# Swapping products between the two rounds of a seven-product down projection

## The chip, the cores and the metric

The kernel runs on one core of a Trainium2 chip: TensorE (PE) for matmuls and transposes, VectorE (DVE), ScalarE (ACT), GpSimd (POOL), and SyncE (SP), whose queue issues most DMAs. The metric is the device time of one execution in microseconds. A profiled execution also has a span, from its first to its last instruction.

## The reference

A decoder block on 512 tokens of width 1024: an RMS norm, one wide input projection, sliding-window attention and a gated linear recurrence side by side, their merge, an output projection with residual, and then the part at issue, a SwiGLU network of hidden width 2816 followed by a last norm:

```python
u = rmsnorm(h, norm_ffn_g[layer])
z = (jax.nn.silu(jnp.einsum('bsd,df->bsf', u, w_ffn_gate[layer]))
     * jnp.einsum('bsd,df->bsf', u, w_ffn_up[layer]))
h = h + jnp.einsum('bsf,fd->bsd', z, w_ffn_down[layer])
return rmsnorm(h, norm_final_g)
```

Everything is float32.

## The kernel before, in words

Every float32 operand is split into a high part in a rounded format (a ScalarE copy, line 109 for weights) and a low part, the rest (a VectorE subtraction, line 113). A product is then three matmuls: high by high, high by low, low by high.

Weights come through the class `Weights`. Its units of 1 MB are loaded into two buffers `raw` (lines 56 to 74), in one fixed list; each unit is two grains, and `get` splits grains two ahead of use into three buffers `wh`/`wl`.

The down projection z (512 x 2816) by w_d (2816 x 1024) is done as a fast 2 x 2 block product: the blocks are the two token halves, two neighbouring blocks of 128 hidden rows (a pair, p = 0 to 10), and the two output halves. Seven products per pair stand in place of eight. Each takes a form of z (a11, a12, a22, and sums s2, s3, n1, n4) and a form of the weights (b11, b12, b21, b22, and sums y1 to y4), and accumulates over the pairs in PSUM. With two token tiles of 128 and three matmuls of 512 columns a product is six matmuls per pair.

Seven products need fourteen PSUM banks and there are eight, so there are two rounds. Round 1, n1y1, a12b21 and n4b22, lies inside the gate/up stream: for each p the list `ffn` (lines 189 to 192) puts two gate projections, the round-1 products of p-1, then two up projections; the products of the last two pairs stand at the end. `up_` (lines 906 to 922) multiplies gate and up, forms the sums of z in `z8` and splits them: three forms (h1, l1) for round 1 at once, four (zh, zl) kept for round 2. Round 2, lines 964 to 983, reads w_d again for a11b11, s3y3, s2y2 and a22y4. `sums` (lines 117 to 128) forms the weight sums in place on VectorE: one per pair in round 1 (y1), three in round 2 (y3, y2, y4).

Between the rounds, lines 950 to 957, ScalarE copies the six banks of round 1 to SBUF and GpSimd adds them onto hn, the residual, in eight additions. Then the pool is released and round 2 takes all eight banks. The last TAIL_P = 2 pairs have their four grains split into buffers of their own (lines 970 and 971) and their matmuls traced product by product (`tail`). Lines 1021 to 1041 add the four results onto hn, take the squares of each row block for the last norm, scale and store.

The order of instructions on each engine is made when the program is built: a scheduler lists them by a simulated timeline, keeping dependences; `tc.issue_after(x)` makes an instruction follow x on its engine. On the chip each engine keeps that order. So matmuls of several products of the tail are mixed in the trace.

Of the kernel before, what the change touches and what calls it, by code (L numbers as in the profile page):

```python
# [22 lines left out]
P = 128  # L23
# [8 lines left out]
C_K, C_V, C_HQ, C_HF, C_HI, C_HG, C_GA, C_GB = (  # L32
    1024, 1152, 1280, 2304, 3328, 4352, 5376, 6400)
NP = NF // 2
TAIL_P = 2
WARM = 28
AHEAD = 2

# [3 lines left out]
class Weights:  # L42
# [13 lines left out]
    def load(self, u):  # L56
        if u >= len(self.units) or u in self.raw:
            return
        kind, w, c0 = self.units[u]
        t = self.pool.tile([P, 2048], F32, tag="raw", bufs=2, name=f"raw{u}")  # L60
        if kind in ("r1", "r2"):
            self.nc.sync.dma_start(
                t.rearrange("p (f n) -> p f n", f=2),
                w[c0 * P:(c0 + 2) * P, :].rearrange("(f p) n -> p f n", p=P))
        elif kind == "n":
            k0, n0 = c0
            self.nc.sync.dma_start(
                t.rearrange("p (k n) -> p k n", k=4),
                w[k0 * P:(k0 + 4) * P, n0:n0 + 512].rearrange("(k p) n -> p k n", p=P))
        else:  # L70
            self.nc.sync.dma_start(
                t.rearrange("p (k n) -> p k n", k=KD),
                w[:, c0:c0 + 256].rearrange("(k p) n -> p k n", p=P))
        self.raw[u] = t
# [10 lines left out]
    def split(self, i, pool=None, bufs=3, high=None, low=None, low_after=None):  # L85
        u, kind, half = self.grans[i]
        self.load(u)
        if u:
            self.load(u + 1)
        nc, raw = self.nc, self.raw[u]  # L90
        if kind == "c":
            src = raw.rearrange("p (k n) -> p k n", k=KD)[:, :, half * P:(half + 1) * P]
            shape = dict(k=KD)
        else:
            n = 256 if kind == "k" else 512
            src = raw[:, half * 1024:(half + 1) * 1024].rearrange("p (k n) -> p k n", n=n)
            shape = dict(n=n)
        size = 1024
        if kind in ("r1", "r2"):
            self.sums(kind, half, raw)  # L100
            if kind == "r1" and not half:
                src, size = src[:, 0:1, :], 512
# [12 lines left out]
        self.done = i + 1  # L115

    def sums(self, kind, half, raw):

        b11, b12, b21, b22 = (raw[:, 512 * i:512 * i + 512] for i in range(4))
        add = lambda o, i0, i1: self.nc.vector.tensor_tensor(o, i0, i1, ALU.add)  # L120
        if kind == "r1":
            if not half:
                add(b11, b11, b12)
        elif not half:
            add(b12, b12, b22)
        else:
            add(b22, b11, b12)
            add(b21, b21, b22)

    def get(self, limit=None):  # L130
        i = self.pos
# [8 lines left out]
def block_kernel(ctx: ExitStack, tc: tile.TileContext, x, norm_mix_g, w_in, b_in,  # L140
# [722 lines left out]
    def psg(name):  # L863
        return psum.tile([P, S], F32, tag="g", bufs=2, name=name)
# [38 lines left out]
    def halves(v):  # L903
        return v.rearrange("p (a c) -> p a c", a=2)

    def up_(p):
        z8 = fp.tile([P, 8, 256], F32, tag="z8", bufs=1, name="z8")
        n1, n4, a12, a11, s2, s3, a22, a21 = (z8[:, i, :] for i in range(8))
        for a in range(2):
            dst = z8.rearrange("p (a b) c -> p a b c", a=2)[:, :, 3 - a, :]  # L910
            tt(dst, halves(fproject()), halves(gates_of[p][a]), ALU.mult)  # L911
            if not a:
                tt(s3, a21, a11, ALU.subtract)
        tt(n1, a21, a22, ALU.subtract)
        tt(s2, a11, n1, ALU.subtract)
        tt(n4, a12, s2, ALU.subtract)
        h1 = fp.tile([P, 3, 256], F32R, tag="h1", bufs=2, name="f1h")
        l1 = fp.tile([P, 3, 256], F32R, tag="l1", bufs=2, name="f1l")
        for h, l, src in ((h1, l1, z8[:, 0:3, :]), (zh[:, p], zl[:, p], z8[:, 3:7, :])):
            act(h, src, AF.Copy)  # L920
            tt(l, src, h.bitcast(F32), ALU.subtract)
        forms1[p] = h1, l1

    def product(ps, ah, al, wh, wl, first, last):
        for i in range(2):
# [3 lines left out]

    def round1(p):  # L930
        h, l = forms1.pop(p)
        for names in (("n1y1",), ("a12b21", "n4b22")):
            wh, wl = W.get(limit=stream_end)
            for b, n in enumerate(names):
                f = dict(n1y1=0, n4b22=1, a12b21=2)[n]
# [23 lines left out]
    psum = newpool("psd", "left", bass.MemoryType.PSUM)  # L959
    acc = {n: [psum.tile([P, S], F32, name=f"{n}_{i}") for i in range(2)]  # L960
           for n in ("a11b11", "s3y3", "s2y2", "a22y4")}
    form = dict(a11b11=0, s2y2=1, s3y3=2, a22y4=3)

    for p in range(NP - TAIL_P):
        for names in (("a11b11", "s3y3"), ("a22y4", "s2y2")):
            wh, wl = W.get(limit=stream_end)
            for b, n in sorted(enumerate(names), key=lambda v: v[1] == "a22y4"):
                product(acc[n], zh[:, p, form[n]], zl[:, p, form[n]], wh[:, b], wl[:, b],
                        p == 0, False)
    for g in range(2 * TAIL_P):  # L970
        W.split(stream_end + 1 + g, wd, 2 * TAIL_P)

    def tail(n, i):

        for p in range(NP - TAIL_P, NP):
            g = stream_end + 1 + 2 * (p - NP + TAIL_P) + (n in ("s2y2", "a22y4"))
            wh, wl = W.ready[g]
            b = int(n in ("s3y3", "s2y2"))
            ts = slice(i * P, (i + 1) * P)
            ah, al = zh[:, p, form[n], ts], zl[:, p, form[n], ts]  # L980
            for m, (x, w) in enumerate(((ah, wh), (ah, wl), (al, wh))):
                pe.matmul(acc[n][i], x, w[:, b], start=False, stop=p == NP - 1 and m == 2)
        return acc[n][i]

    jks = {}
# [1 line left out]
    def start_row(t):  # L987
        s2 = dp.tile([P, 5], F32, tag="s2", bufs=4, name="s2d")
        dve.memset(s2[:, 4:5], EPS)
        jks[t] = s2  # L990
# [30 lines left out]
    vs = []  # L1021
    for i in range(2):
        p1 = tail("a11b11", i)
        start_row(i)
        v = dp.tile([P, S], F32, tag="v", bufs=2, name="v")
        act(v, p1, AF.Copy)
        add_side(i, 0, p1)
        vs.append(v)
    for i in range(2):
        tt(vs[i], tail("s2y2", i), vs[i], ALU.subtract)  # L1030
        add_side(i, 1, vs[i])
        finish_row(i, 1)
    for i in range(2):
        t = 2 + i
        tt(vs[i], tail("s3y3", i), vs[i], ALU.add)
        start_row(t)
        add_side(t, 1, vs[i])
        tt(hn[:, t, 0:S], hn[:, t, 0:S], vs[i], ALU.subtract)
    for i in range(2):
        add_side(2 + i, 0, tail("a22y4", i))  # L1040
        finish_row(2 + i, 0)
    for pl in (dp, zpool, top):
        pl.release()
    for pl in (wd, hpool, wpool, cst):
# [32 lines left out]
```

## Time and profile before

| | us |
|---|---|
| runs | 918.30 median, 917.96 to 920.95 (3 runs) |
| profiled execution, its own time | 919.07 |
| its span | 917.2 |
| PE busy | 885.4 (97%) |
| DVE busy | 554.4 (60%) |
| ACT busy | 398.3 (43%) |
| POOL busy | 163.1 (18%) |
| mean granted TensorE clock | 0.988 of full speed |

Busy is the time in which an engine had an instruction in work; matmuls are pipelined, so a busy PE says that matmuls followed each other, not how fast. The gate/up stream runs from about 541 to 823, round 2 from about 829 to 899, and what follows to 917.2 is the closing of the rows.

### The profile page before, as it was taken

What the parts mean: (1) busy time and instruction counts of PE and PEld (TensorE: products, weight loads), DVE (VectorE), ACT (ScalarE), POOL (GpSimd) and SP (SyncE); (2) the same over time, 40 slices, a digit from 0 to 9 for tenths busy, and PEclk for the clock granted to TensorE, in tenths of its full rate; (3) what the DMA queues carried; (4) which work ended last, traced back from release to release, by engine and by line L of the source; (5) the groups of instructions that cost most, each with busy time, mean ns of one, the idle gap of its engine ahead of it and who ended that gap; (6) DMA issues with size and microseconds to landing.
All of it is one profiled execution on the core that took longest, in us unless ns stands there. A gap on an engine that the chain in (4) does not pass through costs nothing.

```text
span 917.2 us, 11242 instructions
## 1 busy us (share of the span) xinstructions
PE 885.4 (97%) x4410; PEld 747.8 (82%) x4410; DVE 554.4 (60%) x833; ACT 398.3 (43%) x648; POOL 163.1 (18%) x156
## 2 busy tenths in 40 slices
PE   8999999999999999999999999999999999997992
PEld 7888889898888988888888878888888888875881
DVE  5677877556484846545434454555656556467777
ACT  6566766654452726125222343333333323243334
POOL 3013533300000000000000002233333122225004
PEclk9999999999999999999999999999999999999996
DMA  7221211323222131312252222443343333434542
GB/s 255 93 93 47 92 51 43 110 74 113 71 92 85 33 114 60 125 46 93 93 194 94 85 86 92 138 137 102 128 138 95 135 117 113 138 94 138 204 139 91
DMA packets 74465, 97.26 MB, mean 106 GB/s; under 512 B 1866, under 2 KB 64428, under 8 KB 74412
## 3 DMA queue, kind: packets, MB, share of 16 engines
q1 hardware_dynamic: 73820, 95.48, 31.9%
q10 hardware_dynamic: 592, 1.05, 0.3%
q8 instruction: 35, 0.57, 0.3%
q14 instruction: 18, 0.15, 0.0%
HBM read 94.43 MB, written 2.10 MB: 105 GB/s over the span
## 4 chain that ended last, share of the span: by engine, by line
PE 89%; DVE 4%; DMA 3%; SPq 1%; issue 1%; ACT 0%; POOL 0%; POOLq 0%; DVEq 0%; ACTq 0%
PE ps_big L385 13%; PE ps_big L386 13%; PE ps_big L387 13%; PE ps_f L385 8%; PE ps_f L387 8%; PE ps_f L386 8%; DMA raw<-in_w_ffn_down_dram 3%; PE ps_v L396 2%; PE ps_v L397 2%; PE ps_v L395 2%; PE ps_o L396 2%; PE ps_o L397 2%; PE ps_o L395 2%; PE pv L521 1%; PE n4b L928 1%; PE a12b L928 1%
## 5 line engine op out<-in xcount | busy, mean ns | idle before, releaser
L109 ACT ACTIVATE wh<-raw 128x1024 fp32r<-128x1024 f32 (+1 forms) x169 | 174.0, 1032 | 372.8 <-PE ps_f L386 145.9
L113 DVE TENSOR_TENSOR wl<-raw,wh 128x1024 fp32r<-128x1024 f32 (+1 forms) x169 | 211.6, 1253 | 112.0 <-ACT wh L109 111.7
L385 PE MATMUL ps_big<-uh,wh 128*128 128x512 f32 x376 | 148.8, 396 | 0.0
L386 PE MATMUL ps_big<-ul,wh 128*128 128x512 f32 x376 | 147.8, 393 | 0.0
L387 PE MATMUL ps_big<-uh,wl 128*128 128x512 f32 x376 | 147.7, 393 | 0.0
L385 PE MATMUL ps_f<-u2h,wh 128*128 128x512 f32 x352 | 137.1, 390 | 0.8 <-DVE R L880 0.8
L387 PE MATMUL ps_f<-u2h,wl 128*128 128x512 f32 x352 | 137.0, 389 | 0.0
L386 PE MATMUL ps_f<-u2l,wh 128*128 128x512 f32 x352 | 136.9, 389 | 0.0
L387 PEld LDWEIGHTS ps_big<-uh,wl 128*128 128x128 f32 x376 | 70.7, 188 | 14.2
L386 PEld LDWEIGHTS ps_big<-ul,wh 128*128 128x128 f32 x376 | 70.8, 188 | 13.6
L385 PEld LDWEIGHTS ps_big<-uh,wh 128*128 128x128 f32 x376 | 70.7, 188 | 13.5
L385 PEld LDWEIGHTS ps_f<-u2h,wh 128*128 128x128 f32 x352 | 66.1, 188 | 15.1 <-DVE R L880 1.6
L386 PEld LDWEIGHTS ps_f<-u2l,wh 128*128 128x128 f32 x352 | 66.1, 188 | 13.8
L387 PEld LDWEIGHTS ps_f<-u2h,wl 128*128 128x128 f32 x352 | 66.1, 188 | 13.8
L899 POOL TENSOR_TENSOR zg<-zg,sgf 128x512 f32<-128x512 f32 x22 | 37.9, 1723 | 194.2 <-ACT sgf L158 194.2
L120 DVE TENSOR_TENSOR raw<-raw 128x512 f32<-128x512 f32 x44 | 33.7, 765 | 38.8 <-DMA raw<-in_w_ffn_down_dram 38.1
L279 POOL TENSOR_TENSOR r<-ss,neghalf 128x4 f32<-128x4 f32 x8 | 10.1, 1260 | 232.8 <-DVE ss L278 232.8
L911 DVE TENSOR_TENSOR z<-ps_f,zg 128x512 f32<-128x512 f32 x22 | 15.1, 688 | 37.9 <-PE ps_f L387 37.9
L900 POOL TENSOR_TENSOR zg<-zg,R 128x512 f32<-128x512 f32 x22 | 36.7, 1669 | 1.7
L395 PE MATMUL ps_v<-wh,uh 128*128 128x256 f32 x128 | 36.5, 285 | 0.0
L396 PE MATMUL ps_v<-wl,uh 128*128 128x256 f32 x128 | 36.3, 284 | 0.0
L397 PE MATMUL ps_v<-wh,ul 128*128 128x256 f32 x128 | 36.2, 284 | 0.0
(299 smaller groups left out, 1615.8 us busy)
## 6 DMA issues: line engine op xcount, KB each, us to landing
raw<-in_w_in_dram SPq DMA_DIRECT2D x27, 1024.0 KB, 5.2
raw<-in_w_ffn_down_dram SPq DMA_DIRECT2D x22, 1024.0 KB, 4.9
raw<-in_w_ffn_gate_dram SPq DMA_DIRECT2D x11, 1024.0 KB, 5.1
raw<-in_w_ffn_up_dram SPq DMA_DIRECT2D x11, 1024.0 KB, 5.2
raw<-in_w_branch_attn_dram SPq DMA_DIRECT2D x4, 1024.0 KB, 5.3
raw<-in_w_branch_hgrn_dram SPq DMA_DIRECT2D x4, 1024.0 KB, 4.8
raw<-in_w_out_dram SPq DMA_DIRECT2D x4, 1024.0 KB, 4.8
xt<-in_x_dram SPq DMA_DIRECT2D x4, 512.0 KB, 6.5
```

The costliest lines, as they stand in the source:

```text
L109: nc.scalar.activation(hv, src, AF.Copy)
L113: (low or nc.vector).tensor_tensor(lv, src, hv.bitcast(F32), ALU.subtract)
L120: add = lambda o, i0, i1: self.nc.vector.tensor_tensor(o, i0, i1, ALU.add)
L385: pe.matmul(ps, wh[:, k, :], ah[:, k, :], start=k == 0, stop=False)
L386: pe.matmul(ps, wh[:, k, :], al[:, k, :], start=False, stop=False)
L387: pe.matmul(ps, wl[:, k, :], ah[:, k, :], start=False, stop=k == KD - 1)
L395: pe.matmul(ps, ah[:, k0 + k, ts], wh[:, k, :], start=first and k == 0, stop=False)
L396: pe.matmul(ps, ah[:, k0 + k, ts], wl[:, k, :], start=False, stop=False)
L397: pe.matmul(ps, al[:, k0 + k, ts], wh[:, k, :], start=False, stop=last and k == nk - 1)
L899: pool_e.tensor_tensor(zg, zg, sg, ALU.mult)
L900: pool_e.tensor_tensor(zg, zg, R, ALU.mult)
L928: pe.matmul(ps[i], x[:, ts], w, start=first and n == 0, stop=last and n == 2)
```

## The change

Round 1 now computes s3y3, a22y4 and s2y2, whose weights need three sums per pair; round 2 computes a11b11, n1y1, a12b21 and n4b22, which need one. The weight rows of round 2 are loaded as single blocks of 128 rows, two DMAs of 512 KB per unit, so that for the last three pairs (TAIL_P = 3) the three even blocks come first, then the odd ones. The round-1 products of pair 9 move between the gate and up projections of pair 10; those of pair 10 follow the last up projection directly, and for that pair the forms of z are split one by one. Between the rounds eight GpSimd additions become ten on VectorE. bc, the broadcast of the row scale, uses a bank of s2y2. The products of the tail are tied to the order in which they are traced, accumulator by accumulator, and the closing of the rows follows that order.

```diff
-TAIL_P = 2
+TAIL_P = 3
...
+        elif kind == "r2":
+            for i, r in enumerate(c0):
+                self.nc.sync.dma_start(t[:, D * i:D * i + D], w[r * P:r * P + P, :])
...
+        kind, _, rows = self.units[u]
+        x = [raw[:, 512 * i:512 * i + 512] for i in range(4)]
         add = lambda o, i0, i1: self.nc.vector.tensor_tensor(o, i0, i1, ALU.add)
-        if kind == "r1":
-            if not half:
-                add(b11, b11, b12)
+        if kind == "r2":
+            if rows[half] % 2 == 0:
+                add(x[2 * half + 1], x[2 * half], x[2 * half + 1])
         elif not half:
-            add(b12, b12, b22)
+            add(x[1], x[1], x[3])
         else:
-            add(b22, b11, b12)
-            add(b21, b21, b22)
+            add(x[3], x[0], x[1])
+            add(x[2], x[2], x[3])
...
-        ffn += [("g", p)] + ([("d", p - 1)] if 0 < p < NP - 1 else []) + [("u", p)]
-    ffn += [("d", NP - 2), ("d", NP - 1)]
+        ffn += [("g", p)] + ([("d", p - 1)] if p else []) + [("u", p)]
+    ffn += [("d", NP - 1)]
...
-    units += [("r2", w_d, 2 * p) for p in range(NP)]
+    rows2 = list(range(NF - 2 * TAIL_P))
+    rows2 += list(range(NF - 2 * TAIL_P, NF, 2)) + list(range(NF - 2 * TAIL_P + 1, NF, 2))
+    units += [("r2", w_d, tuple(rows2[i:i + 2])) for i in range(0, NF, 2)]
...
-    bc = psg("ps_bc")
     rounds1 = {n: [psum.tile([P, S], F32, name=f"{n}_{i}") for i in range(2)]
-               for n in ("n1y1", "a12b21", "n4b22")}
+               for n in ("s3y3", "a22y4", "s2y2")}
+    bc = rounds1["s2y2"][1]
...
+        place(0)
+        tt(s3, a21, a11, ALU.subtract)
+        if p < NP - 1:
+            place(1)
+            tt(n1, a21, a22, ALU.subtract)
+            tt(s2, a11, n1, ALU.subtract)
+            split(h1, l1, z8[:, 4:7, :])
+        else:
+            split(h1[:, 2], l1[:, 2], s3)
+            place(1)
+            split(h1[:, 0], l1[:, 0], a22)
+            tt(n1, a21, a22, ALU.subtract)
+            tt(s2, a11, n1, ALU.subtract)
+            split(h1[:, 1], l1[:, 1], s2)
+        tt(n4, a12, s2, ALU.subtract)
+        split(zh[:, p], zl[:, p], z8[:, 0:4, :])
...
-    for n, places in (("n1y1", ((0, 1), (2, 1))), ("a12b21", ((0, 0),)),
-                      ("n4b22", ((0, 1),))):
-        for i in range(2):
-            ev = dp.tile([P, S], F32, tag="ev", bufs=6, name="ev")
-            act(ev, rounds1[n][i], AF.Copy)
-            for t, side in places:
-                dst = hn[:, t + i, sides[side]]
-                pool_e.tensor_tensor(dst, dst, ev, ALU.add)
+    evs = []
+    for i in range(2):
+        ev = dp.tile([P, S], F32, tag="ev", bufs=2, name="ev")
+        act(ev, rounds1["s3y3"][i], AF.Copy)
+        evs.append(ev)
+    for i in range(2):
+        onto(2 + i, 0, rounds1["a22y4"][i])
+    for i in range(2):
+        onto(i, 1, rounds1["s2y2"][i])
+        tt(evs[i], rounds1["s2y2"][i], evs[i], ALU.add)
+    for i in range(2):
+        onto(2 + i, 1, evs[i])
+        onto(2 + i, 0, evs[i], ALU.subtract)
...
+        with tc.issue_after(order["last"]) if order["last"] else nullcontext():
+            for p in range(NP - TAIL_P, NP):
...
+                    ins = pe.matmul(acc[n][i], x, w[:, b], start=False,
+                                    stop=p == NP - 1 and m == 2)
+        order["last"] = raw_ins(ins)
...
+        onto(2 + i, 1, p1, ALU.subtract)
+        onto(i, 1, p1, ALU.subtract)
+        onto(i, 0, p1)
+        y = hn[:, 2 + i, 0:S]
+        pool_e.tensor_tensor(y, y, v, ALU.add)
+        for c in range(2):
+            square(2 + i, c)
     for i in range(2):
+        w1 = tail("n1y1", i)
+        add_side(2 + i, 1, w1)
+        onto(i, 1, w1)
+        finish_row(2 + i, 1)
+    for i in range(2):
+        add_side(i, 0, tail("a12b21", i))
+        add_side(i, 1, tail("n4b22", i))
         finish_row(i, 1)
```

`onto(t, side, src, op)` is one VectorE operation of 128x512 on hn; `add_side` is two additions of 128x256, each followed by a square on ScalarE; `finish_row` multiplies by the norm's gain on GpSimd, reduces the squares, takes the power on GpSimd, scales and stores.

## Rows read from the trace of the kernel before

**Rows 1.** Busy time by stretch: stretch, length, each engine's busy us (count), clock, DMA share, GB/s

```profile
700.00:800.00 100.00, 100.00 (x443) 82.81 (x442) 55.04 (x63) 32.96 (x38) 28.20 (x16) 1.00 0.39 126
...
840.00:850.00 10.00, 4.71 (x11) 3.74 (x12) 7.47 (x5) 1.97 (x2) 4.15 (x3) 0.72 0.37 124
...
870.00:880.00 10.00, 10.00 (x46) 8.28 (x45) 8.55 (x10) 3.53 (x4) 0.00 (x0) 1.00 0.51 176
```

**Rows 2.** Chain of waits in the gate/up stream: start us, us, what

```profile
756.60 1.36 PE n1y L928 x6
757.96 1.36 PE a12b L928 x6
```

**Rows 3.** Waits of TensorE from 480 on: total us, times, longest us

```profile
PE s2y L928 <- DVE wl L113: 6.2, 2, 5.6
PE n1y L928 <- ACT f1h L153: 2.0, 1, 2.0
PE ps_f L385 <- DVE R L880: 0.8, 1, 0.8
```

**Rows 4.** Timeline of VectorE between the rounds: start us, us, instruction, idle before

```profile
819.27 0.69 DVE L911 TENSOR_TENSOR z<-ps_f,zg 128x512 f32<-128x512 f32 x1 [3.15 <-PE ps_f L387]
...
820.48 0.42 DVE L914 TENSOR_TENSOR z<-z 128x256 f32<-128x256 f32 x1
...
828.85 2.14 DVE L120 TENSOR_TENSOR raw<-raw 128x512 f32<-128x512 f32 x3 [0.84 <-DMA raw<-in_w_ffn_down_dram]
...
830.95 2.29 DVE L113 TENSOR_TENSOR wl<-raw,wh 128x1024 fp32r<-128x1024 f32 x1
...
838.14 4.89 DVE L120 TENSOR_TENSOR raw<-raw 128x512 f32<-128x512 f32 x3 [2.67 <-DMA raw<-in_w_ffn_down_dram]
```

**Rows 5.** VectorE's groups from 851 to 888: count, busy us, mean ns, idle before

```profile
L113 DVE TENSOR_TENSOR wl<-raw,wh 128x1024 fp32r<-128x1024 f32 x14 | 17.1, 1222 | 5.5 <-ACT wh L109 5.4
L120 DVE TENSOR_TENSOR raw<-raw 128x512 f32<-128x512 f32 x21 | 14.5, 690 | 1.0 <-DMA raw<-in_w_ffn_down_dram 0.5
```

**Rows 6.** Timeline of GpSimd between the rounds

```profile
830.51 13.64 POOL L957 TENSOR_TENSOR hn<-hn,ev 128x512 f32<-128x512 f32 x8 [17.15 <-ACT ev L153]
```

**Rows 7.** Timeline of TensorE: after its longest wait, and its last matmul

```profile
845.29 0.79 PE L928 MATMUL s2y<-wl,zh 128*128 128x512 f32 x1 [5.59 <-DVE wl L113]
...
851.00 0.48 PE L928 MATMUL a11b<-wh,zl 128*128 128x512 f32 x1
...
898.73 0.39 PE L982 MATMUL a22y<-wh,zl 128*128 128x512 f32 x1
```

**Rows 8.** Timeline of VectorE in the tail

```profile
896.46 0.76 DVE L1001 TENSOR_TENSOR hn<-a11b,hn 128x256 f32<-128x256 f32 x2 [4.52 <-ACT v L153]
...
905.93 1.35 DVE L1016 TENSOR_SCALAR hn<-hn,r1d 128x256 f32<-128x256 f32 x1
...
909.26 1.40 DVE L1001 TENSOR_TENSOR hn<-a22y,hn 128x256 f32<-128x256 f32 x4
...
912.87 0.35 DVE L1016 TENSOR_SCALAR hn<-hn,r1d 128x256 f32<-128x256 f32 x1
913.14 0.48 DVE L1017 SCALAR_TENSOR_TENSOR hn<-hn,r1d,gfin 128x256 f32<-128x256 f32 x1
```

**Rows 9.** Timeline of VectorE, low part of the second round-1 weight grain

```profile
752.12 1.23 DVE L113 TENSOR_TENSOR wl<-raw,wh 128x1024 fp32r<-128x1024 f32 x1 [0.23 <-ACT wh L109]
```

**Rows 10.** Loads: the four of hn by tile (issues, landing), and w_ffn_down's from the page

```profile
L811 SPq DMA_DIRECT2D hn<-in_x_dram x4: 340/428/432, 471.1 to 472.4; - x4
...
DMA to landing us min/median/max: 4.6/5.3/6.1
...
raw<-in_w_ffn_down_dram SPq DMA_DIRECT2D x22, 1024.0 KB, 4.9
```

**Rows 11.** Timeline of ScalarE in round 2

```profile
843.14 1.06 ACT L109 ACTIVATE wh<-raw 128x1024 fp32r<-128x1024 f32 x1 [2.23 <-DVE raw L120]
```

**Rows 12.** Timeline of GpSimd in the tail

```profile
912.24 0.60 POOL L1014 TENSOR_TENSOR r1d<-s1d,neghalf 128x1 f32<-128x1 f32 x1
```

More of the change, by code (lines that the diff above doesn't have):

```diff
@@ L60, in load @@
         t = self.pool.tile([P, 2048], F32, tag="raw", bufs=2, name=f"raw{u}")
-        if kind in ("r1", "r2"):
+        if kind == "r1":
             self.nc.sync.dma_start(
@@ L99, in split @@
         if kind in ("r1", "r2"):
-            self.sums(kind, half, raw)
+            self.sums(u, half, raw)
             if kind == "r1" and not half:
-                src, size = src[:, 0:1, :], 512
+                src, size = src[:, 1:2, :], 512
         pool = pool or self.pool
@@ L115, in split, with sums @@
         self.done = i + 1
-    def sums(self, kind, half, raw):
-        b11, b12, b21, b22 = (raw[:, 512 * i:512 * i + 512] for i in range(4))
+    def sums(self, u, half, raw):
+        kind, _, rows = self.units[u]
+        x = [raw[:, 512 * i:512 * i + 512] for i in range(4)]
         add = lambda o, i0, i1: self.nc.vector.tensor_tensor(o, i0, i1, ALU.add)
-        if kind == "r1":
-            if not half:
-                add(b11, b11, b12)
+        if kind == "r2":
+            if rows[half] % 2 == 0:
+                add(x[2 * half + 1], x[2 * half], x[2 * half + 1])
         elif not half:
-            add(b12, b12, b22)
+            add(x[1], x[1], x[3])
         else:
-            add(b22, b11, b12)
-            add(b21, b21, b22)
+            add(x[3], x[0], x[1])
+            add(x[2], x[2], x[3])
     def get(self, limit=None):
@@ L907, in up_, with split, place @@
         z8 = fp.tile([P, 8, 256], F32, tag="z8", bufs=1, name="z8")
[L908 to L919, printed above, removed]
+        a12, n1, n4, a11, a22, s2, s3, a21 = (z8[:, i, :] for i in range(8))
+        h1 = fp.tile([P, 3, 256], F32R, tag="h1", bufs=1, name="f1h")
+        l1 = fp.tile([P, 3, 256], F32R, tag="l1", bufs=1, name="f1l")
+        forms1[p] = h1, l1
+        def split(h, l, src):
             act(h, src, AF.Copy)
             tt(l, src, h.bitcast(F32), ALU.subtract)
-        forms1[p] = h1, l1
+        def place(a):
+            dst = z8.rearrange("p (a b) c -> p a b c", a=2)[:, :, 0 if a else 3, :]
+            tt(dst, halves(fproject()), halves(gates_of[p][a]), ALU.mult)
+        place(0)
[14 more added lines that the diff above has]
+        split(zh[:, p], zl[:, p], z8[:, 0:4, :])
     def product(ps, ah, al, wh, wl, first, last):
@@ L931, in round1 @@
         h, l = forms1.pop(p)
-        for names in (("n1y1",), ("a12b21", "n4b22")):
+        for names in (("s3y3",), ("a22y4", "s2y2")):
             wh, wl = W.get(limit=stream_end)
             for b, n in enumerate(names):
-                f = dict(n1y1=0, n4b22=1, a12b21=2)[n]
+                f = dict(a22y4=0, s2y2=1, s3y3=2)[n]
                 product(rounds1[n], h[:, f], l[:, f], wh[:, b], wl[:, b],
@@ L949, in block_kernel, with onto @@
     sides = (slice(0, S), slice(S, D))
-    for n, places in (("n1y1", ((0, 1), (2, 1))), ("a12b21", ((0, 0),)),
-                      ("n4b22", ((0, 1),))):
-        for i in range(2):
-            ev = dp.tile([P, S], F32, tag="ev", bufs=6, name="ev")
-            act(ev, rounds1[n][i], AF.Copy)
-            for t, side in places:
-                dst = hn[:, t + i, sides[side]]
-                pool_e.tensor_tensor(dst, dst, ev, ALU.add)
+    def onto(t, side, src, op=ALU.add):
+        dst = hn[:, t, sides[side]]
+        tt(dst, dst, src, op)
+    evs = []
[11 more added lines that the diff above has]
+        onto(2 + i, 0, evs[i], ALU.subtract)
     psum.release()
@@ L960, in block_kernel @@
     acc = {n: [psum.tile([P, S], F32, name=f"{n}_{i}") for i in range(2)]
-           for n in ("a11b11", "s3y3", "s2y2", "a22y4")}
-    form = dict(a11b11=0, s2y2=1, s3y3=2, a22y4=3)
+           for n in ("a11b11", "n1y1", "a12b21", "n4b22")}
+    form = dict(a12b21=0, n1y1=1, n4b22=2, a11b11=3)
     for p in range(NP - TAIL_P):
-        for names in (("a11b11", "s3y3"), ("a22y4", "s2y2")):
+        for names in (("a11b11", "n1y1"), ("a12b21", "n4b22")):
             wh, wl = W.get(limit=stream_end)
-            for b, n in sorted(enumerate(names), key=lambda v: v[1] == "a22y4"):
+            for b, n in enumerate(names):
                 product(acc[n], zh[:, p, form[n]], zl[:, p, form[n]], wh[:, b], wl[:, b],
@@ L971, in block_kernel @@
         W.split(stream_end + 1 + g, wd, 2 * TAIL_P)
+    order = dict(last=None)
     def tail(n, i):
[L975 to L982, printed above, removed]
+        with tc.issue_after(order["last"]) if order["last"] else nullcontext():
+            for p in range(NP - TAIL_P, NP):
+                g = stream_end + 1 + p - NP + TAIL_P + TAIL_P * (n in ("a12b21", "n4b22"))
+                wh, wl = W.ready[g]
+                b = int(n in ("n1y1", "n4b22"))
+                ts = slice(i * P, (i + 1) * P)
+                ah, al = zh[:, p, form[n], ts], zl[:, p, form[n], ts]
+                for m, (x, w) in enumerate(((ah, wh), (ah, wl), (al, wh))):
+                    ins = pe.matmul(acc[n][i], x, w[:, b], start=False,
+                                    stop=p == NP - 1 and m == 2)
+        order["last"] = raw_ins(ins)
         return acc[n][i]
@@ L1019, in finish_row @@
             q.dma_start(out2[t * P:(t + 1) * P, hs], y[:, hs])
-    vs = []
     for i in range(2):
@@ L1024, in block_kernel @@
         start_row(i)
-        v = dp.tile([P, S], F32, tag="v", bufs=2, name="v")
+        start_row(2 + i)
+        v = dp.tile([P, S], F32, tag="ev", bufs=2, name="v")
         act(v, p1, AF.Copy)
-        add_side(i, 0, p1)
-        vs.append(v)
-    for i in range(2):
-        tt(vs[i], tail("s2y2", i), vs[i], ALU.subtract)
-        add_side(i, 1, vs[i])
-        finish_row(i, 1)
[L1033 to L1041, printed above, removed]
+        onto(2 + i, 1, p1, ALU.subtract)
[5 more added lines that the diff above has]
+            square(2 + i, c)
+    for i in range(2):
+        w1 = tail("n1y1", i)
[5 more added lines that the diff above has]
+        add_side(i, 1, tail("n4b22", i))
+        finish_row(i, 1)
     for pl in (dp, zpool, top):
```

## The prediction

> **What bounds the kernel now.** I read the busy shares by stage first. In the gate/up stream TensorE is busy for the whole of a 100 us stretch at full granted clock while VectorE is at 55% [rows 1]. A product of six matmuls takes 1.36 us, 0.227 us from start to start [rows 2], and the change leaves the number of matmuls as it is, so a gain can only come from places where TensorE stands still or runs at half clock. The waits of TensorE in the second half of the span name three [rows 3]: 2.0 us before the last round-1 product, 6.2 us in two waits for a low weight part at the start of round 2, and 0.8 us for R. The stretch 840 to 850 shows the second: TensorE 4.71 of 10 us busy, granted clock 0.72 [rows 1].
>
> The timelines say why. At 828 to 847 VectorE does sums and low parts of round-2 weights at up to twice their normal time: three sums in 4.89 us where three took 2.14, and a low part in 2.29 [rows 4], against means of 0.690 and 1.222 later [rows 5]. Beside it GpSimd runs its eight additions onto hn, 13.64 us from 830.51 [rows 6]. After the 5.6 us wait TensorE is in its lower level, 1.2 GHz: thirteen start-to-start steps from 845.29 to 851.00 take 5.71 us [rows 7] instead of 13 x 0.227 = 2.95, a loss of 2.8. So the passage from round 1 to round 2 loses 2.0 + 6.2 + 2.8 = 11.0 us. Last, the final matmul starts at 898.73 and ends at 899.12 [rows 7], and the span ends at 917.2: 18.1 us of tail in which VectorE, ScalarE and GpSimd close four row blocks. The scheduler has mixed the last products of all accumulators, so VectorE's first addition onto hn starts only at 896.46 [rows 8], 2.7 us before TensorE ends.
>
> **The change part by part.** The sum is made against the profiled execution, 919.07 us (span 917.2 and 1.9 around it); the median of the runs is 0.8 less.
>
> *Sums moved into the stream.* Round 1 gets two sums more per pair, round 2 two fewer. 22 sums x 0.690 = 15.2 us of VectorE work enter the stream, 1.4 us per pair of 25.84 us (18 matmuls of products and 96 of projections, 114 x 0.2267). Cover: VectorE is idle 45% there, and the low part of the second round-1 weight ends at 753.35 [rows 9] while its first matmul is at 757.96 [rows 2], 4.6 us later. Two sums cost 1.4 us, or 3.3 at the 1.63 that they take beside GpSimd [rows 4], and GpSimd works on the gates there. I take nothing; the lower bound is nothing too, as TensorE has no idle time to give back, the upper is all 15.2 (a rival below).
>
> *Round 2 lighter.* Per pair VectorE does one sum and two low parts, 0.690 + 2 x 1.222 = 3.1 us, instead of 4.5, in TensorE's 24 x 0.227 = 5.44. TensorE is already full there (10.00 of 10 us at 870 to 880 [rows 1]), so this gives nothing there; it lets VectorE catch up after the passage.
>
> *Loads in halves.* Each round-2 load of 1 MB becomes two of 512 KB: eleven more issues on SP's queue, behind which only later loads wait. Nearest row: four 512 KB loads issued within 1.8 us landed 4.6 to 6.1 us after their issue [rows 10], so 2 MB came in under 8 us, and a pair should be in after about 5, as the single load is now (the first half sooner, and the sum needs only that). With two buffers TensorE waits only when a pair takes over 2 x 5.44 - (0.69 + 1.06 + 2 x 1.22) = 6.7 us [rows 5, 11]. I take nothing; the bound is 2 x 5.3, the two in series. The Trainium skill (DMA: Bandwidth & Descriptors, Anatomy of one DMA) speaks against halves: a fixed 2 us for each DMA, whatever its size, fitted to DMAs issued from GpSimd. By it a pair in series would take an estimated 6.4 us where one load takes 4.4, still under the limit just worked out, so the sum would be the same; the four overlapping loads show that the fixed part isn't paid in series.
>
> *Passage between the rounds.* GpSimd's eight additions and four of six ScalarE copies go; ten additions of 128x512 come to VectorE, in front of the weight work of round 2. The slow-down by GpSimd goes with them. What is late next is VectorE's own backlog. Between the end of the last up projection and the low part that the second pair needs, VectorE has: one gating product 0.69, five subtractions of 0.42 [rows 4], one 128x1024 low part of z 1.22, ten additions at 0.69 (the 128x512 row), two sums 1.38 and three low parts 3.67: about 15.9 us. TensorE's work in that time is 18 + 24 matmuls, 9.5 us. If all of it stands in front, TensorE is 6.4 us late; if the scheduler leaves the last four additions and the z low part for later (nothing needs them soon), 2.4. Most of the program order speaks for the adds in front, readiness speaks for the weights. I take the middle, 4.4, and 0.6 for the last round-1 products, which now follow the up projection directly and wait for a chain of product, copy and subtraction (s3, prepared early, covers 1.36 of it). So 5.0 us lost in place of 11.0: gain 6.0. Ends: 2.0 lost (gain 9.0), or 6.4 + 0.6 and once more 2.8 at half clock, 9.8 lost (gain 1.2).
>
> *The tail.* Now nine matmuls, 2.04 us, per accumulator, in fixed order, eight accumulators one after another. The closing work can start 14 us before TensorE ends instead of 2.7. VectorE's share: six additions for the a11b11 pair, 4.1; two halves and one addition each for n1y1, 2.8; four times 0.70 for the other two [rows 8], 2.8; four row ends of reduce, scale and scale-multiply, about 1.0 each, 4.0; and the last three low parts, 3.7: 17.4 in TensorE's 16.3, beginning some 2 us after it. So VectorE ends 3 us after TensorE, which the last row needs anyway: additions 0.70, square, reduce, power on GpSimd 0.60 [rows 12], scale and multiply 0.35 + 0.48 [rows 8], 3.2 with the square at an estimated 0.6 (ScalarE's 1.06 for 1024 columns [rows 11], cut to 256 with its readout) and the handovers. From the end of the last multiply to the span's end it is 917.2 - 913.6 = 3.6 now [rows 8]. That makes 6.8; 1.2 more for scales that meet GpSimd (1.35 instead of 0.35 at 905.93 [rows 8]): 8.0 in place of 18.1, gain 10.1. Against it: the first accumulator needs row block 20 at its seventh matmul, 1.4 us into the tail. Its load starts when pair 7's buffer is free, some 5.7 us before the tail, and then 4.9 landing, 0.69, 1.06 and 1.22 follow: ready 2.3 us in. With a fixed order nothing can pass it: 0.9 lost. Net 9.2; ends 5 (row ends that VectorE can't keep up with, four at +1 us) and 11.
>
> *bc in a bank of its own.* The second gate projection no longer shares a bank with bc: 0.8 us [rows 3]. The other end is a loss of 2.8, four evacuations of 0.69, if the projection's bank is now one that still holds transposed blocks. I take the gain, as it is what the row shows.
>
> Sum: 919.07 - 6.0 - 9.2 - 0.8 = 903.1, and 0.8 less beside the median: 902.5 rounded.
>
> **Rivals.** *A, the backlog is paid in full and the tail half* (20%): the ten additions stand before the weights, one long wait brings the half clock back, and the row ends pile up on VectorE. 919.07 - 1.2 - 5 - 0.8 = 912. For it: 15.9 against 9.5 us, and the scheduler did place sums that waited for a load ahead of a ready low part at 838 [rows 4]. Against: most of the additions are needed by nobody soon.
> *B, both go as well as they can* (12%): 919.07 - 9.0 - 11 - 0.8 = 898. For it: without GpSimd beside it VectorE's rows are as short as in 852 to 888.
> *C, slower: the halved loads run in series* (5%): a pair takes 2 x 5.3 = 10.6 us, two buffers turn over in (10.6 + 0.69 + 1.06 + 2.44) / 2 = 7.4 us, TensorE waits 2.0 in each of eleven pairs: 21.5 us, 924. It outweighs the gains from 1.5 us per pair, a pair of loads of about 9.7 us. Against it: the four loads that overlap [rows 10].
> *D, the sums aren't hidden in the stream* (4%): 15.2 us come back there, 903.1 + 15.2 = 918, no change. For it: sums are slower beside GpSimd [rows 4]; against: the 4.6 us of slack.
>
> **How the numbers follow.** The forecast has 59%, its own range 898 to 908. The range of 8 in 10 takes in B's lower part and A: 895 to 912. What can be told from no change is 0.3%, 2.8 us. Faster: forecast, A, B and a bit of D, 0.91; same, most of D, 0.03; slower: C and contended sums, 0.06.
>
> **What would show it.** Right: no GpSimd addition at 830 to 844, waits of TensorE between the rounds of 3 to 7 us in several short pieces, the clock at 1.0 there; stream pairs still 25.84 us apart; the accumulators ending 2.04 us apart; 7 to 9 us from the last matmul to the end; the wait for R gone. Wrong: pairs of the stream further apart, waits for round-2 loads in every pair, one wait over 4 us with half clock behind it, or a tail over 12 us.

## The result, and the profile after

The changed kernel takes 911.15 us (median of 4 runs, 909.97 to 911.42) against 918.73 for the kernel before run beside it: ratio 0.991 with an interval of 0.989 to 0.993. So it gains 7.6 us, where 16 were forecast. The profiled execution is 911.42, its span 909.7 (917.2 before), and the two traces, compared stage by stage, show where the missing gain went.

First the busy shares by stretch of the changed kernel (columns as in [rows 1]):

```profile
700.00:800.00 100.00, 100.00 (x443) 82.81 (x442) 60.86 (x74) 32.91 (x39) 28.20 (x16) 1.00 0.39 125
...
820.00:830.00 10.00, 7.03 (x27) 4.67 (x26) 6.47 (x11) 3.14 (x5) 0.00 (x0) 0.90 0.31 105
830.00:840.00 10.00, 6.28 (x14) 4.51 (x15) 8.42 (x19) 3.20 (x4) 0.00 (x0) 0.50 0.47 159
840.00:850.00 10.00, 10.00 (x42) 8.16 (x42) 4.77 (x6) 3.18 (x3) 0.00 (x0) 0.92 0.29 105
870.00:880.00 10.00, 10.00 (x46) 8.29 (x45) 6.59 (x7) 4.55 (x5) 0.00 (x0) 1.00 0.49 164
```

In the stream VectorE does eleven instructions more per 100 us (74 against 63, 60.86 us busy against 55.04 [rows 1]) and TensorE stays full with the same 443 matmuls. In round 2 it is full at full clock too. Between the rounds it isn't: from 830 to 840 it has 14 matmuls in work, at a granted clock of 0.50. Its waits from 480 on (us in total, times, longest; compare [rows 3]):

```profile
PE a11b L948 <- ACT ev L157: 3.7, 1, 3.7
PE a22y L948 <- ACT f1h L157: 2.1, 1, 2.1
PE px L845 <- DVE hn L842: 0.8, 1, 0.8
PE a11b L1014 <- DVE wl L116: 0.8, 1, 0.8
PE s2y L948 <- ACT f1h L157: 0.7, 1, 0.7
PE a22y L948 <- DVE f1l L921: 0.2, 1, 0.2
```

The wait for R is gone (the px wait was there before as well), the waits of 6.2 and 2.0 us between the rounds too; in their place stand 3.7 + 2.1 + 0.7 + 0.2 = 6.7 us between the rounds and 0.8 in the tail. TensorE's timeline, against [rows 7], first where the gate/up stream begins:

```profile
541.84 0.47 PE L391 MATMUL ps_f<-u2h,wh 128*128 128x512 f32 x1
...
823.01 0.39 PE L948 MATMUL s3y<-wh,f1h 128*128 128x512 f32 x1
...
829.91 0.80 PE L948 MATMUL s2y<-wh,f1h 128*128 128x512 f32 x1 [0.70 <-ACT f1h L157]
...
836.56 0.80 PE L948 MATMUL a11b<-wh,zh 128*128 128x512 f32 x1 [3.72 <-ACT ev L157]
...
844.51 0.39 PE L948 MATMUL a11b<-wh,zh 128*128 128x512 f32 x1
...
900.07 0.39 PE L1014 MATMUL n4b<-wh,zl 128*128 128x512 f32 x1
```

From 823.01 to 844.51 TensorE does 42 matmuls (18 of round 1, 24 of round 2), 9.5 us of work, in 21.5: 12.0 us lost. I call this stretch the passage. The kernel before, where the stream begins, before its first wait and where it is back at full pace:

```profile
540.85 0.47 PE L385 MATMUL ps_f<-u2h,wh 128*128 128x512 f32 x1
...
822.85 0.39 PE L928 MATMUL n4b<-wh,f1l 128*128 128x512 f32 x1
...
852.71 0.63 PE L928 MATMUL s2y<-wh,zh 128*128 128x512 f32 x2
```

Its passage begins one step after the second row, at 823.08: the 78 matmuls from there to 852.71 lose 29.63 - 78 x 0.2267 = 11.95. (The prediction's 11.0 counted waits and half clock, not the slow starts around the waits.) The two are equal: the passage gained nothing. Of the 12.0, 6.7 are waits and 3.6 half clock (the six s2y and the twelve matmuls from 836.56 are 0.425 us apart instead of 0.227); the rest, 1.7, stands at the single starts around the waits. The repeat of the changed kernel below loses 11.4 there, so differences of half a us in the passage mean nothing.

VectorE's timeline in the passage, against [rows 4], and one row of ScalarE's:

```profile
824.84 0.69 DVE L124 TENSOR_TENSOR raw<-raw 128x512 f32<-128x512 f32 x1 [3.53 <-DMA raw<-in_w_ffn_down_dram]
825.45 0.68 DVE L925 TENSOR_TENSOR z<-ps_f,zg 128x512 f32<-128x512 f32 x1
...
832.85 0.69 DVE L124 TENSOR_TENSOR raw<-raw 128x512 f32<-128x512 f32 x1 [1.58 <-DMA raw<-in_w_ffn_down_dram]
833.46 1.28 DVE L973 TENSOR_TENSOR hn<-hn,s2y 128x512 f32<-128x512 f32 x2
834.66 1.22 DVE L921 TENSOR_TENSOR zl<-z,zh 128x1024 fp32r<-128x1024 f32 x1
```
```profile
835.91 1.09 ACT L157 ACTIVATE ev<-s3y 128x512 f32<-128x512 f32 x2 [1.93 <-DVE zl L921]
```

VectorE isn't overloaded there: it stands idle for 5.1 us with a weight sum of round 2 at the head of its queue whose load hasn't landed. Behind the first of them waits the last gating product (its projection's last matmul started at 822.78), on which the last forms of z and so a22y4 and s2y2 hang. Behind the second wait the additions of s2y and the low part of z; and the copies of s3y3 (ev) wait for that low part, because the ev tiles lie where z8 was. a11b11 takes the bank of s3y3 and waits for the copy.

The tail, on VectorE (against [rows 8]):

```profile
889.04 3.67 DVE L973 TENSOR_TENSOR hn<-hn,a11b 128x512 f32<-128x512 f32 x6
...
900.97 1.35 DVE L1050 TENSOR_SCALAR hn<-hn,r1d 128x256 f32<-128x256 f32 x1 [0.77 <-POOL r1d L1048]
902.24 0.47 DVE L1051 SCALAR_TENSOR_TENSOR hn<-hn,r1d,gfin 128x256 f32<-128x256 f32 x1
902.64 0.74 DVE L1035 TENSOR_TENSOR hn<-n4b,hn 128x256 f32<-128x256 f32 x2
...
904.93 0.35 DVE L1050 TENSOR_SCALAR hn<-hn,r1d 128x256 f32<-128x256 f32 x1 [0.75 <-POOL r1d L1048]
905.20 0.48 DVE L1051 SCALAR_TENSOR_TENSOR hn<-hn,r1d,gfin 128x256 f32<-128x256 f32 x1
```

The first addition onto hn starts 11.4 us before TensorE's end (900.46) instead of 2.7. From TensorE's end to the span's end it is 9.24 us, 18.1 before.

The spans are accounted for: passage 0.0, tail 18.1 - 9.24 = 8.9 less 1.4 that TensorE loses inside it (the 0.8 us wait at 885.43 and the slow starts around it), the gate/up stream 1.06 (the wait for R, 0.8, and the slow starts behind it), and a first stream matmul that started 1.0 later (541.84 against 540.85; in the repeat of the changed kernel it is at 541.23 and over all runs at 540.7 to 541.8, so this is not the change's): 8.9 - 1.4 + 1.06 - 1.0 = 7.6, against 917.2 - 909.7 = 7.5.

### The profile page after: what moved, and what is told of

It reads as the page before. It is cut to its first block, busy times and chain, and to the rows that moved or that the text cites. A ratio compares the mean times of both kernels' runs of the same rounds, so it can differ in the third digit from the quotient of the medians.

```text
span 909.7 us, 11255 instructions
## 1 busy us (share of the span) xinstructions
PE 887.8 (98%) x4410; PEld 749.0 (82%) x4410; DVE 556.6 (61%) x843; ACT 396.6 (44%) x646; POOL 153.4 (17%) x150
## 4 chain that ended last, share of the span: by engine, by line
PE 87%; DMA 5%; DVE 4%; SPq 1%; issue 1%; ACT 1%; POOL 0%; DVEq 0%; POOLq 0%; ACTq 0%
PE ps_big L391 13%; PE ps_big L392 13%; PE ps_big L393 13%; PE ps_f L391 8%; PE ps_f L392 8%; PE ps_f L393 8%; DMA raw<-in_w_ffn_down_dram 4%; DVE wl L116 2%; PE ps_v L402 2%; PE ps_v L403 2%; PE ps_v L401 2%; PE ps_o L402 2%; PE ps_o L403 2%; PE ps_o L401 2%; PE pv L527 1%; PE s2y L948 1%
## 5 line engine op out<-in xcount | busy, mean ns | idle before, releaser
L902 DVE TENSOR_TENSOR zg<-ps_f,R 128x512 f32<-128x512 f32 x22 | 15.2, 692 | 37.9 <-PE ps_f L393 37.9
```

Of the source, the lines that this page charges most:

```text
L902: tt(zg, fproject(row_scale if p == 0 and a == 0 else None), R, ALU.mult)
```

## The experiments

All ratios are to the kernel before, run beside each on the same chip. The changed kernel itself, repeated as `after_again`, had 910.02 us, ratio 0.991 (0.989 to 0.993), with the same waits (a11b 3.7, a22y 2.0, a11b in the tail 0.7).

> The kernel after once more, as the measure for the kernels beside it. Its ratio to the kernel before should come out near 0.991 again; if tail_free's 0.9888 was the removed wait of 0.8 us and little else, this stays 1 to 2 us above it.

**Sums behind the low part (`sum_order`).** My theory: not the amount of VectorE's work but its order, a sum that waits for a load ahead of ready work, sets the passage.

```diff
-            self.sums(u, half, raw)
+            with self.tc.issue_after(self.low) if kind == "r2" else nullcontext():
+                self.sums(u, half, raw)
...
-            (low or nc.vector).tensor_tensor(lv, src, hv.bitcast(F32), ALU.subtract)
+            ins = (low or nc.vector).tensor_tensor(lv, src, hv.bitcast(F32), ALU.subtract)
+        self.low = getattr(ins, "ins", ins)
```

> The kernel after, with each round-2 weight sum kept behind the low part of the grain before it on VectorE. Theory (a sum that waits for its load stands at the head of VectorE's queue, in front of the gating product at 824.84 and of s2y2's additions and the z low part at 832.85): the 2.1 us wait before a22y4 falls under 0.7, the 3.7 us wait before a11b11 under 2, the half clock goes or shortens; 904 to 907 us, 4 to 8 less than the kernel after. Rival (VectorE simply has more work there than fits, 15.9 us against 9.5): the waits only move; less than 2 us gained.

Measured: 906.82, ratio 0.988 (0.986 to 0.989), 3.3 us under the changed kernel by the ratios. VectorE's gating product and TensorE's waits:

```profile
822.62 0.69 DVE L928 TENSOR_TENSOR z<-ps_f,zg 128x512 f32<-128x512 f32 x1 [2.22 <-PE ps_f L396]
```
```profile
PE s2y L951 <- DVE f1l L924: 2.0, 1, 2.0
PE a11b L951 <- ACT ev L159: 1.7, 1, 1.7
```

The product is no longer held: counted from the first s3y matmul of the passage it starts 2.2 us earlier (0.26 behind it instead of 2.44). The wait of a22y falls from 2.1 to 0.3, that of a11b from 3.7 to 1.7; that of s2y grows from 0.7 to 2.0. The six s2y now run at full clock, the twelve matmuls behind the wait of a11b still at half. The passage (822.36 to 839.67) loses 7.8 instead of 12.0. Work and loads are the same, so the order was worth about 4 us there; behind the passage TensorE loses 0.6 more than in the changed kernel (2.0 against 1.4).

**The copies in memory of their own (`ev_apart`).**

```diff
-        ev = dp.tile([P, S], F32, tag="ev", bufs=2, name="ev")
+        ev = wd.tile([P, S], F32, tag="ev", bufs=2, name="ev")
...
-        v = dp.tile([P, S], F32, tag="ev", bufs=2, name="v")
+        v = wd.tile([P, S], F32, tag="ev", bufs=2, name="v")
```

> The kernel after, with the two SBUF tiles that take the copies of s3y3 in a place of their own instead of z8's. Theory (the copies wait for the z low part because they are written where z8 was, and a11b11 waits for its bank): the copies start right after the weight copy at 834.0 instead of 835.9, a11b11 1.9 us earlier; 909 to 910 us. Rival (a11b11's start is set by VectorE's additions or by the weights of round 2): the wait keeps its length under another name, 911.

Measured: 908.22, ratio 0.989 (0.986 to 0.991), a little under the 909 to 910 expected. The copies no longer wait for the low part of z; counted from the first s3y matmul (822.33 here) they start 2.2 us earlier. TensorE's wait for them falls by 2 us, and the passage (822.33 to 842.08) loses 10.2 instead of 12.0:

```profile
833.02 1.06 ACT L157 ACTIVATE ev<-s3y 128x512 f32<-128x512 f32 x2
```
```profile
PE a22y L948 <- ACT f1h L157: 1.9, 1, 1.9
PE a11b L948 <- ACT ev L157: 1.7, 1, 1.7
```

**No fixed order in the tail (`tail_free`).** The theory here was mine from the prediction: the fixed order of the last products brings the gain of the tail.

```diff
-        with tc.issue_after(order["last"]) if order["last"] else nullcontext():
+        with nullcontext():
```

> The kernel after without the fixed order of the last products. Theory (the fixed order is what lets the closing of the rows start early): a11b11 and n1y1 are mixed again, the first addition onto hn comes some 2 us later and the tail after the last matmul grows by 1 to 3 us; 912 to 914. Rival (the order in which the weights come, even blocks first, and the new last products do it): within 1 us of the kernel after; or a little faster, as TensorE needs not wait 0.8 us for row block 20.

Measured: 908.11, ratio 0.989 (0.987 to 0.991), and 8.6 us from TensorE's end to the span's. TensorE's last matmul, in a span of 906.9:

```profile
897.88 0.39 PE L1014 MATMUL n4b<-wh,zl 128*128 128x512 f32 x1
```

The theory fell: without the fixed order the tail is as short, and the wait of 0.8 us in it is gone.

**Plain order of the row blocks (`rows_plain`).** No fixed order, and also the last three pairs loaded pair by pair, so that a11b11 can't close before the last loads.

```diff
-    rows2 = list(range(NF - 2 * TAIL_P))
-    rows2 += list(range(NF - 2 * TAIL_P, NF, 2)) + list(range(NF - 2 * TAIL_P + 1, NF, 2))
+    rows2 = list(range(NF))
...
-                g = stream_end + 1 + p - NP + TAIL_P + TAIL_P * (n in ("a12b21", "n4b22"))
+                g = stream_end + 1 + 2 * (p - NP + TAIL_P) + (n in ("a12b21", "n4b22"))
```

> The kernel after without the fixed order of the last products and with the weight rows of round 2 in plain order (even and odd block of a pair together, as before the change), still three pairs in the tail. Theory (the early even blocks are what lets a11b11 and n1y1 finish first): the last products are mixed again, the first addition onto hn comes later than 4 us before TensorE ends, and the time after the last matmul goes from 9 back to 13 to 18 us; 913 to 918. Rival (the new products and their cheaper closing do it): within 2 us of tail_free.

Measured: 912.9, ratio 0.995 (0.993 to 0.996): 5.2 slower than `tail_free` by the ratios. The first additions of a11b11 wait for their product and start 6.1 us before TensorE's end (897.12), not within 4 us as expected, and 13.2 us remain after it:

```profile
890.99 3.68 DVE L972 TENSOR_TENSOR hn<-hn,a11b 128x512 f32<-128x512 f32 x6 [2.94 <-ACT v L157]
```

So 4.6 of the tail's gain is the even blocks coming first (13.2 to 8.6). The other 4.9 (18.1 to 13.2) belong to the swapped products with their cheaper closing and to the third tail pair, which no run separates.

**The kernel before with its sums tied (`before_sum_order`, `before_one_sum`).** If the order of the sums is the cause, it should cost the kernel before as well. The first edit is that of `sum_order` in the kernel before; the second ties only the sums of the first grain of the third round-2 unit (`if u - self.first2 == 2 and not half`).

> The kernel before, with each round-2 weight sum kept behind the low part of the grain before it on VectorE. Theory (the 5.6 us wait was the order: three sums that waited for a load stood ahead of a low part that was ready): that wait falls to 0 to 2.5, the half clock behind it goes, 912 to 915 us, 4 to 7 less than the kernel before. Rival (GpSimd's eight additions slow VectorE, in whatever order): 917 to 918.

> The kernel before with one edit in the order: the sums of the third round-2 unit stand behind the low part of the second unit's second grain on VectorE, nothing else is tied. Theory (those three sums, waiting for their load at 838, held the low part that TensorE wanted): the 5.6 us wait falls under 2.5 and the half clock goes with it; 4 to 7 us less than the kernel before, 911 to 914. Rival (GpSimd's additions slow VectorE so that it is late in any order): under 2 us gained.

`before_sum_order` measured 926.33, ratio 1.009 (1.007 to 1.010). The tie was too wide: it put each grain's sums behind the low part of the grain before in all eleven units, and TensorE now waits eight times for a high part (5.0 us in total). So it can't tell what the passage alone would gain. `before_one_sum` measured 915.9, ratio 0.998 (0.997 to 0.999), about 2 us instead of the 4 to 7 expected. The long wait is halved, 5.6 to 2.6 us, but the sums and low parts are as slow as in [rows 4]:

```profile
PE a11b L932 <- DVE wl L114: 2.6, 1, 2.6
```
```profile
838.88 4.69 DVE L122 TENSOR_TENSOR raw<-raw 128x512 f32<-128x512 f32 x3 [0.42 <-DMA raw<-in_w_ffn_down_dram]
843.50 4.50 DVE L114 TENSOR_TENSOR wl<-raw,wh 128x1024 fp32r<-128x1024 f32 x2
```

GpSimd, whose additions the change removed, is busy for all of 840 to 845 here. In the profiled execution (915.85) the passage, 823.96 to 849.28, loses 7.6 instead of 11.95, so there the order was worth 4.3; 0.9 of that went in a stream that began later (541.74 against 540.85). Over the ten runs about 2 remain. So the order costs the kernel before as well, but isn't all; GpSimd beside VectorE is the likely rest, which no run isolates.

**The passage repaired (`passage`, `passage_free`).** `passage` ties the sums of the second and third round-2 unit, gives ev a pool of its own, and puts a22y's additions behind the low part of s2. For the last pair n4 and the split of the kept forms (`marks["keep"]`) come after the additions of s2y. `passage_free` takes the fixed order of the tail out as well.

```diff
+            with self.tc.issue_after(self.low) if 0 < u - self.first2 < 3 else nullcontext():
+                self.sums(u, half, raw)
...
-        ev = dp.tile([P, S], F32, tag="ev", bufs=2, name="ev")
+        ev = evp.tile([P, S], F32, tag="ev", bufs=2, name="ev")
...
-    for i in range(2):
-        onto(2 + i, 0, rounds1["a22y4"][i])
+    with tc.issue_after(marks["s2"]):
+        for i in range(2):
+            onto(2 + i, 0, rounds1["a22y4"][i])
...
+    marks["keep"]()
```

> The kernel after with four edits in the passage: the sums of the second and third round-2 unit behind the low part of the grain before, the two copies of s3y3 in a place of their own and traced ahead of the kept forms of the last pair, a22y4's additions behind the low part of s2, and the split of the kept forms later. Theory (the passage is lost by order and by places of tiles, not by the amount of work on VectorE): the waits between the rounds add up to under 2 us, the granted clock stays at 1.0, 5 to 8 us less than sum_order's gain aside: 898 to 902. Rival (15.9 us of VectorE work in 9.5 us of TensorE's): waits of 4 us or more remain, under other names; 905 to 907.

> The kernel passage (sums tied to the grain before, ev tiles in a pool of their own, a22y additions behind s2's low part) without the fixed order of the last products. Theory: the fixed order makes TensorE wait in the tail for VectorE's sums (1.9 + 0.8 us at 876.27 and 877.53 in passage, and 2 to 3 us at half clock behind them), and brings nothing in return, since without it the changed kernel was as fast at the end (8.6 us against 9.2 from the last matmul to the end). So the waits in the tail go and the time is 900 to 903, 2 to 5 us under passage. Rival: the last weight sums come late by VectorE's own work, in whatever order the products stand; then TensorE waits as long in another place, and the time is 904 to 906, the same as passage.

`passage` measured 904.97, ratio 0.986 (0.985 to 0.988). Between the rounds two short waits remain, 0.7 and 0.3, the granted clock is 1.00 there, and the passage loses 834.08 - 822.35 - 42 x 0.2267 = 2.2 us, though VectorE has the same work as in the changed kernel:

```profile
822.35 0.39 PE L959 MATMUL s3y<-wh,f1h 128*128 128x512 f32 x1
...
834.08 0.62 PE L959 MATMUL a11b<-wh,zh 128*128 128x512 f32 x2
```

The rival that its 15.9 us of work are the bound is out. But the expected 898 to 902 wasn't reached: in the tail the fixed order now has TensorE wait for weight parts of a11b11.

```profile
876.27 0.49 PE L1028 MATMUL a11b<-wh,zh 128*128 128x512 f32 x1 [1.89 <-ACT wh L113]
877.53 0.79 PE L1028 MATMUL a11b<-wl,zh 128*128 128x512 f32 x1 [0.77 <-DVE wl L117]
...
880.68 0.43 PE L1028 MATMUL a11b<-wh,zl 128*128 128x512 f32 x1
```

`passage_free` measured 901.75, ratio 0.982 (0.980 to 0.984), inside its 900 to 903; all its waits from 480 on are these:

```profile
PE px L849 <- DVE hn L846: 0.8, 1, 0.8
PE s2y L959 <- DVE f1l L925: 0.8, 1, 0.8
PE a22y L959 <- DVE f1l L925: 0.3, 1, 0.3
```

TensorE ends at 889.29 instead of 894.05; 0.4 of that is a stream that began earlier, the other 4.3 is what it lost in the tail under the fixed order. Part of that comes back: 10.8 us to the span's end instead of 8.25.

**Whole loads (`one_load`, `one_load_free`).** The eight units of two neighbouring row blocks become one DMA of 1 MB again, in the changed kernel and in `passage_free`.

```diff
-        if kind == "r1":
+        if kind == "r1" or kind == "r2" and c0[1] == c0[0] + 1:
+            r = c0 if kind == "r1" else c0[0]
...
-                w[c0 * P:(c0 + 2) * P, :].rearrange("(f p) n -> p f n", p=P))
+                w[r * P:(r + 2) * P, :].rearrange("(f p) n -> p f n", p=P))
```

> The changed kernel with the eight round-2 units of two neighbouring row blocks loaded as one DMA of 1 MB again; the six units of the last three pairs keep their order, and those whose rows aren't neighbours keep two DMAs of 512 KB. Theory: the halves cost TensorE nothing in round 2, which was full at full clock at 850 to 880; between the rounds they matter only through the load that the 3.53 and 1.58 us of waiting at 824.84 and 832.85 are for. With one load of 1 MB (4.8 us to landing against 4.2 for a half) the sums come 0.6 us later at most: 910 to 912, no change against the changed kernel's 910.6. Rival: the second DMA of a pair is paid in series (by the Trainium skill, DMA: Bandwidth & Descriptors, Anatomy of one DMA, an estimated 2 us a pair); then those two waits shrink by about 2 us each and the time is 907 to 908.

> The same edit in passage_free, where no sum at the head of VectorE's queue waits between the rounds. Theory: loads are off TensorE's path there, so the time stays at 901 to 902.5. Rival, the halves in series: 898 to 900.

`one_load` measured 905.85, ratio 0.986 (0.984 to 0.988), 4.4 us under the changed kernel by the ratios; `one_load_free` 899.8, ratio 0.980 (0.978 to 0.981). My expectation of no change is wrong by these, and the second time lies in the rival's 898 to 900, but the rival's mechanism isn't what the trace shows. VectorE in `one_load`:

```profile
822.38 0.69 DVE L926 TENSOR_TENSOR z<-ps_f,zg 128x512 f32<-128x512 f32 x1 [0.99 <-PE ps_f L394]
...
826.05 0.69 DVE L125 TENSOR_TENSOR raw<-raw 128x512 f32<-128x512 f32 x1 [0.71 <-DMA raw<-in_w_ffn_down_dram]
```

Counted from the first s3y matmul (822.11 here, 823.01 in the changed kernel), the whole load released its sum after 3.9 us, later than the halves did (1.8). But the gating product now stands ahead of that sum, and runs 2.2 us earlier (after 0.3 instead of 2.4). The passage (822.11 to 840.42) loses 8.8 instead of 12.0, and the tail has no wait. So the edit of the load's size changed the order in which the scheduler lists VectorE's work; that it does so by its own estimate of the landing is argued, not shown. In `one_load_free` the passage loses 2.2 as before; TensorE ends 0.3 later and the tail takes 8.3 instead of 10.8 us. The shorter tail can be read from VectorE, first in `passage_free`, then in `one_load_free`:

```profile
874.42 0.69 DVE L126 TENSOR_TENSOR raw<-raw 128x512 f32<-128x512 f32 x1 [0.97 <-DMA raw<-in_w_ffn_down_dram]
```
```profile
871.26 0.69 DVE L127 TENSOR_TENSOR raw<-raw 128x512 f32<-128x512 f32 x1 [0.77 <-DMA raw<-in_w_ffn_down_dram]
```

The last sum's load lands 3.2 us earlier, the additions onto hn begin 1.9 earlier (879.39 against 881.30), and as VectorE has nearly no idle time from there on, its last multiply begins 1.9 earlier too (893.78 against 895.67). In `one_load` the same load (row block 20) lands 1.9 us before the second matmul of the tail, in the changed kernel 0.6 before, which fits the wait that is gone. Why these loads come earlier is open.

## Why the prediction was half right

*Sums hidden in the stream: right.* From the first ps_f matmul to the end of pair 9's round-1 products and pair 10's projections, in whichever order, it is 281.17 us, 282.23 before; the wait for R (0.8) and the slow starts behind it are the difference, so 22 sums cost nothing.

*Bank for bc: right*, 0.8, and 1.06 with the slow starts.

*Round 2 lighter: right*, nothing there; VectorE waits for loads before six of seven sums (10.2 us from 847 to 882), TensorE doesn't.

*Loads in halves: nothing as a transfer, not nothing as an edit.* The landing of the round-2 loads, from the page of the changed kernel (the first line is round 1's):

```profile
raw<-in_w_ffn_down_dram SPq DMA_DIRECT2D x11, 1024.0 KB, 4.8
raw<-in_w_ffn_down_dram SPq DMA_DIRECT2D x22, 512.0 KB, 4.2
```

The 4.2 is the middle of two sorts: the first half of a pair lands 3.6 to 3.9 us after its issue, the second 4.5 to 4.8, and as it is issued 0.4 after the first, a pair is in about 5.0 us after its first issue, as predicted, where a whole takes 4.8. So the pair overlaps and rival C is out. TensorE never waited for a load in the steady part of round 2. The Trainium skill (DMA: Bandwidth & Descriptors, Anatomy of one DMA) gives each DMA, fitted to those issued from GpSimd, a fixed 2 us beside a part that goes by the bytes; by its figures half the bytes would save an estimated 1.2 us. The rows agree nearly: the first half lands some 1.1 us sooner than a whole. What I missed is that the edit moved VectorE's order: with whole loads the passage loses 3.2 us less (`one_load`).

*Passage: wrong, the step that failed.* I took 5.0 us lost and measured 12.0, beyond my upper end of 9.8. I summed VectorE's work (15.9 us) against TensorE's (9.5) as if VectorE were busy throughout and only the amount mattered. With the same work in another order, and ev in memory of its own, 2.2 are lost (`passage`). In the changed kernel VectorE was idle for 5.1 us behind sums that waited for loads, TensorE waited for VectorE's and ScalarE's products in three places, and the half clock cost 3.6, which I had put at nothing in the middle of the range (the sign of being right was a clock of 1.0 there; it was 0.50 from 830 to 840). The profile held the hint, a sum waiting 2.67 us for its load ahead of low parts [rows 4]; I used it only as a point in favour of rival A. The memory of ev, reused from z8, I hadn't looked at: 2 us (`ev_apart`).

*Tail: nearly right in size, wrong in cause.* 9.24 us instead of 8.0, and 1.4 instead of 0.9 lost inside it: gain 7.5 instead of 9.2. VectorE reaches the last n4b addition 2.2 us after TensorE's end (I had allowed 1.2), behind a scale of 1.35; the row's own end, addition to multiply, takes 3.0 (3.2 predicted), and 4.0 follow to the span's end (3.6). But I credited the fixed order, and `tail_free` shows that it brings nothing in the changed kernel; where the passage is repaired it shortens the time after TensorE's end by 2.6 us and costs 4.3 before it (`passage` against `passage_free`). The early even blocks bring 4.6.

So of the forecast gain of 16.0, 6.0 are missing in the passage and 1.7 in the tail, 1.0 is the later start, and the stream gave 0.3 more. The time of 911 is that of rival A, with half its mechanism: one long wait and the half clock did come, but not from ten additions in front of the weights, and the tail was worth 7.5, not 5. That 911 lies inside 895 to 912 is therefore luck in part: the range reached so far up for rival A's price, not for a sum that stands waiting for its load.

## What to carry to other kernels

When work moves to an engine whose queue is in order, don't only add up its instructions: find for each one that waits for a load what stands behind it, and who waits for that. Order and placement were worth as much here as the whole change: 8.4 us from the changed kernel to `passage_free` by the ratios, against 8.2 for the change. The best version, with whole loads, takes 899.8. And an edit of a load's size can change the order in which a scheduler lists everything else, so compare the order first and explain the transfer afterwards.

## What the runs showed of the hardware

Where TensorE goes into a wait at full clock, the lower level shows in the matmuls after the wait. In `passage` the waits of 1.89 and 0.77 us are followed by six steps of about 0.427 us from 878.12 on. In `rows_plain` a wait of 4.5 us lies in the first stretch below (length 5 us, TensorE busy 0.80), with a granted clock of 1.00; the lower level shows in the stretch after it, in which TensorE works again:

```profile
830.00:835.00 5.00, 0.80 (x3) 0.30 (x2) 3.47 (x6) 2.23 (x3) 0.00 (x0) 1.00 0.42 169
835.00:840.00 5.00, 4.54 (x13) 3.66 (x14) 4.56 (x11) 0.90 (x2) 0.00 (x0) 0.66 0.28 105
```

In the changed kernel, whose s2y already ran at the lower level, the granted clock is 0.50 over the wait of 3.7 us too (832.9 to 836.5). And not every wait brings it: the waits of 1.7 and 1.2 us earlier in `rows_plain` are followed, after one slower step of 0.33 to 0.34 us each, by steps of 0.23 to 0.24 us.

A wait can therefore be paid twice: for `one_load`, 4.7 us of waits between the rounds and, from 832.21, a start of 0.60 and eleven steps of 0.427 at the lower level, 1.2 GHz (2.2 us above eleven of 0.227).
